# A two-layer fp32 trunk on one core: the first weights in six pieces on two DMA queues, and tiles that begin at multiples of 128 bytes

## The chip, the cores and the metric

One core of one Trainium2 chip runs the whole kernel. The metric is device microseconds of one execution, as the median of several runs. The core has a matmul engine (TensorE, "PE", with a weight loader "PEld"), VectorE ("DVE"), ScalarE ("ACT"), GpSimd ("POOL") and SyncE ("SP"), which here only issues DMAs. ACT and POOL issue some DMAs too; an engine works through its own instructions, DMA issues among them, in order.

## What is computed

The reference runs 512 tokens of width 1024 through two layers, in float32. Cut to what matters:

```python
def reference(x, ...):
    h = x
    for layer in range(2):
        mix = even_mixer(h, ...) if layer % 2 == 0 else odd_mixer(h, ...)
        h = layer_norm(ALPHA * h + mix, ...)
        h = layer_norm(ALPHA * h + conv_ffn(h, ...), ...)
    return h

def even_mixer(x, ...):
    q_a, k_a, v_a, z_a, b_a, a_a, q_b, k_b, v_b = split(x @ w_in)   # the gates b_a, a_a: 6 + 6 columns
    q_a, k_a, v_a = silu(causal_depthwise_conv(q_a, k_a, v_a))
    beta = sigmoid(b_a)
    g = -exp(a_log) * softplus(a_a + dt_bias)                       # then summed along each chunk
    o_a = rms_norm(gated_delta_rule(l2(q_a), l2(k_a), v_a, g, beta)) * silu(z_a)
    o_b = dilated_attention(q_b, k_b, v_b, rel_bias)
    return concat(o_a, o_b) @ w_out
```

The odd layer has differential attention and gated linear attention in place of these; each layer ends in a convolutional feed-forward (2816 wide).

## The kernel before, in words

Activations lie transposed in SBUF, 128 features by 512 tokens in each of eight blocks: `h` (float32) and its split into a high and a low half in a reduced format, `xh` and `xl` (their names in the trace too). Weights come as 216 units of 512 KB in HBM (`wts`), each 128 x 1024, that is eight blocks of 128 x 128. A unit is loaded into a raw buffer `wr` (three of them), cast on ACT into the high half `wh`, and DVE subtracts to get the low half `wl`. A product is then 8 x 3 matmuls into one PSUM bank `pd`: `xh*wh`, `xl*wh`, `xh*wl`.

Unit 0 holds the columns of the gates (64 of 128 wide, so it is loaded as 64 columns a block, 256 KB, and its low halves lie in the same tile `wh` beside the high ones). Units 1 to 3 are the key, query and value columns of the first head; unit 4 and up follow.

`setup` loads tokens and units 0 and 1 in pieces. `START` lists the pieces in order: `("x", a, e)` is token block a; `(u, a, e)` is blocks a to e of unit u. Before, all token pieces are issued by SP and all weight pieces by ACT. A second loop over the same list casts and subtracts piece by piece. Units 2 and 3 are asked for after that (`self.ask`, which issues on SP), then `par` (per-feature parameters) and `con` (constants, with the identity). Unit 3 goes into the raw buffer of unit 0, unit 4 into that of unit 1, unit 5 into that of unit 2, and so on: a load waits until DVE has made the low half of the unit that lay there.

`even` then interleaves the matmuls of units 0 and 1 block by block (`narrow` and `mm3`), so PE needs the token blocks one after another. After that come units 2, 3, ... (`tile_of`, 24 matmuls each). Beside them the gates' chain runs (`gates`): ACT copies the second gate rows out of PSUM, DVE adds the first; identity, Abs, Exp and Ln on ACT; a max-and-add on DVE; Exp on ACT; scaling and a scan on DVE; then four small transposes `pg` on PE. These lines record their instructions through one helper (L159 before), so they all carry its line. A framework's scheduler sets the order of each engine's instructions; DMAs of SP and ACT take eight completion semaphores in turn.

Scratch tiles of the two mixers (2 KB a partition, tags `x0`, `x1`, ...) come from a pool in which tiles lie one behind another in the order in which they are first asked for. In the kernel before, `idle` (4 bytes) and `par` (1984 bytes) shift what follows them by 32 and 96 bytes, and small tiles of the mixers shift the scratch behind them: in the even mixer scratch begins 32 or 96 bytes past a multiple of 128, in the odd one at a multiple or 64 past it. `h`, `xh`, `xl`, `wr`, `wh`, `wl` and the tiles of the feed-forward begin at multiples of 128 already.

Of the kernel before, what the change touches and what calls it, by code (L numbers as in the profile page):

```python
# [9 lines left out]
F32 = mybir.dt.float32  # L10
# [7 lines left out]
P = 128  # L18
S = 512
# [15 lines left out]
_NP = 0  # L35
# [23 lines left out]
for _n, _w in (("ident", 128), ("maskT", 128), ("nm1", 32), ("i32", 32), ("lm", 4 * 32), ("scan", 512),  # L59
# [30 lines left out]
EVEN_SEQ = "h0 h1 h2 h3 h4 h5 q00 v0 q01 v1 q02 v2 q10 q11 q12 z0 z1 z2 z3 z4 z5"  # L90
ODD_SEQ = "0D12G3abcd"

START = (("x", 0, 1), (0, 0, 4), ("x", 1, 2), (1, 0, 2), ("x", 2, 3), (1, 2, 5), ("x", 3, 4), (0, 4, 8), ("x", 4, 5),
         ("x", 5, 6), (1, 5, 8), ("x", 6, 7), ("x", 7, 8))
WARM = 8
LEAD = 3
AHEAD = 2
# [17 lines left out]
class Chain:  # L115
    def __init__(self, gen, ready, prio):
        self.gen, self.ready, self.prio, self.eng, self.end = gen, ready, prio, None, ready
# [48 lines left out]
class Scratch:  # L166


    def __init__(self, t, pool, n, more=None):
        self.t, self.pool, self.free, self.of = t, pool, list(range(n)), {}  # L170
        if more is not None:
            self.free += [(k, more) for k in range(more.shape[1])]

# [21 lines left out]
class Trunk:  # L195
# [14 lines left out]
    def setup(self):  # L210
        nc, tc, ctx = self.nc, self.tc, self.ctx
        self.keep = ctx.enter_context(tc.tile_pool(name="keep", bufs=1))
        self.wp = ctx.enter_context(tc.tile_pool(name="wp", bufs=1))
        self.psd = ctx.enter_context(tc.tile_pool(name="psd", bufs=4, space=PSUM))
        self.pss = ctx.enter_context(tc.tile_pool(name="pss", bufs=4, space=PSUM))
        keep = self.keep
        self.h = keep.tile([P, KD, S], F32, name="h")
        self.xh = keep.tile([P, KD, S], F32R, name="xh")
        self.xl = keep.tile([P, KD, S], F32R, name="xl")
        first = [(u, self.wtiles()) for u in (U_AB, U_AB + 1)]  # L220

        self.ones = keep.tile([P, P], F32, name="ones")
        nc.gpsimd.memset(self.ones, 1.0 / P)
        idle = keep.tile([P, 1], F32, name="idle")
        tc.keep_in_program_order(nc.scalar.copy(out=idle, in_=self.ones[:, 0:1]))
        for what, a, e in START:
            if what == "x":
                nc.sync.dma_start(self.h[:, a, :], self.xt[:, a, :])
            else:

                u, w = first[what]
                n = 64 if u in NARROW else P
                tc.keep_in_program_order(nc.scalar.dma_start(w[0][:, a * n : e * n], self.wts[u][:, a * n : e * n]))
        self.par = keep.tile([P, _NP], F32, name="par")
        self.con = keep.tile([P, _NCC], F32, name="con")

        warm = self.sps("warm")
        for _ in range(WARM):
            nc.tensor.matmul(warm[:, 0:P], lhsT=self.ones, rhs=self.ones, start=True, stop=True)
        self.onesL = keep.tile([P, P], F32, name="onesL")  # L240
        nc.gpsimd.memset(self.onesL, 1.0 / D)
        self.onesP, self.onesK = (keep.tile([P, P], F32R, name=f"ones{i}") for i in "PK")
        for x, n in ((self.onesP, P), (self.onesK, 512)):
            nc.vector.tensor_scalar(out=x, in0=self.ones, scalar1=P / n, scalar2=None, op0=ALU.mult)
        self.cst = keep.tile([P, 3], F32, name="cst")
        self.one, self.lneps, self.gdneps = (self.cst[:, i : i + 1] for i in range(3))
        nc.gpsimd.memset(self.one, 1.0)
        nc.gpsimd.memset(self.lneps, LN_EPS)
        self.rep = tc.dram_tile([4, P, L_TAB], F32, name="rep")
        self.chains, self.rec, self.asked = [], [], {}  # L250
        self.V, self.A = Eng(self, "DVE", nc.vector), Eng(self, "ACT", nc.scalar)
        self.G, self.T = Eng(self, "POOL", nc.gpsimd), Eng(self, "PE", nc.tensor)
        self.enter(EVEN)
        for what, a, e in START:
            if what == "x":
                hi, lo = self.xh[:, a, :], self.xl[:, a, :]
                nc.scalar.copy(out=hi, in_=self.h[:, a, :])
                nc.vector.tensor_tensor(out=lo, in0=self.h[:, a, :], in1=hi.bitcast(F32), op=ALU.subtract)
            else:
                u, w = first[what]  # L260
                self.split(u, *w, nc.scalar, nc.vector, slice(a * P, e * P))
        for u, w in first:
            self.pre[u] = w[1:]
        for u in (U_AB + 2, U_AB + 3):
            self.ask(u)
        nc.sync.dma_start(self.par, self.par_d)
        nc.sync.dma_start(self.con, self.con_d)
        self.ident = self.c("ident")
# [483 lines left out]
    def even(self):  # L752
        nc, tc = self.nc, self.tc
# [7 lines left out]
        def t1(n, w, bufs):  # L761
            return mp.tile([P, w], F32, name=self.nm(n), tag=n, bufs=bufs)

        self.enter(EVEN)
        g = {"zero": t1("zero", 1, 1)}
        seq = EVEN_SEQ.split()

        def of(x):
            a, i = x[0], int(x[1])
            if a == "h":  # L770
                return range(U_GDN + 3 * i, U_GDN + 3 * i + 3)
            if a == "q":
                u = U_SWA + 6 * i + 2 * int(x[2])
                return range(u, u + 2)
            if a == "v":
                return range(U_SWA + 12 + 2 * i, U_SWA + 14 + 2 * i)
            return range(U_Z + i, U_Z + i + 1)
# [101 lines left out]
        for x in seq:  # L879
            u, i = of(x)[0], int(x[1])  # L880
# [366 lines left out]
    def swa_pair(self, pair, taken, vts, bg, o, mp, t1):  # L1247
# [12 lines left out]
        for g in range(3):  # L1260
# [3 lines left out]
            for hh in range(2):  # L1264
# [3 lines left out]
                for n in range(NCH):  # L1268
                    w = 256 if g == 0 and n > 0 else P
                    if n == 0 or (g == 0 and n == 2):  # L1270
                        while X.room() < 1:
                            yield None
                        x = X.get("sc")
# [20 lines left out]
        def rows(cols, rw):  # L1294

            pr = self.sps("rows")
            T.transpose(out=pr[0:24, 0:P], in_=cols, identity=self.ident)
            tr = t1("tr", P, 2)
            V.tensor_copy(out=tr[0:24, :], in_=pr[0:24, 0:P])
            for hh in range(2):  # L1300
                G.dma_start(rw[hh : hh + 1, :], tr[12 * hh : 12 * hh + 12, :])
            yield 2500
# [5 lines left out]
        yield 0  # L1308
        rw = mp.tile([2, 3 * S], F32, name=self.nm("rw"), tag="rw", bufs=1)
        yield from rows(mx, rw)  # L1310
        while X.room() < 1:
            yield None
# [12 lines left out]
        for g in range(3):  # L1325
            for hh in range(2):
                for n in range(NCH):
                    ci = (g * NCH + n) * 2 + hh
                    li = hh * 12 + g * NCH + n
                    dst, k0, w = sc[g, hh][n]  # L1330
# [3 lines left out]
        for g in range(3):  # L1334
# [4 lines left out]
            for hh in range(2):  # L1339
                blocks = [(n, k0 // P + i, dst[:, i * P : (i + 1) * P]) for n in range(NCH)  # L1340
                          for dst, k0, w in (sc[g, hh][n],) for i in range(w // P)]
                for a in range(0, len(blocks), 4):
# [8 lines left out]
                    w = len(part) * P  # L1351
# [5 lines left out]
            for n in range(NCH):  # L1357
                for i in range(len(pts[0, n])):
                    for hh in range(2):
# [6 lines left out]
                        vt, f = (vts[g][pair], kb * P) if g else (vts[g][kb // 2], kb % 2 * HS + P * pair)  # L1366
# [5 lines left out]
        if pair:  # L1372
            X.put(*(x for v in vts for x in v))
        rw = mp.tile([2, 3 * S], F32, name=self.nm("rw"), tag="rw", bufs=1)
        yield from rows(ls, rw)
        while X.room() < 1:
            yield None
# [625 lines left out]
```

## Time and profile before

| | us |
|---|---|
| median of 3 runs (1410.32 to 1410.57) | 1410.34 |
| the profiled execution | 1412.89 |
| span in its trace, first to last instruction | 1411.1 |
| PE busy | 1385.7 |
| DVE busy | 839.3 |
| ACT busy | 673.5 |

The trace is of one execution, 2.55 us longer than the median of the runs. Busy times of PE count pipelined matmuls, each from its own start to its end, so a busy PE need not be at its peak; a step between starts is shorter than one matmul lasts.

### The profile page before, as it was taken

To read this page: it belongs to the slowest core of one execution; us is meant where nothing else is said; L and a number is where in the kernel's file an instruction comes from. 1 tells how busy PE (TensorE), PEld (TensorE's weight loads), DVE (VectorE), ACT (ScalarE), POOL (GpSimd) and SP (SyncE) were. 2 spreads that over 40 slices of the span, in tenths; PEclk is the share of its full clock that TensorE was granted. 3 is DMA by queue.
4 is the path that set the end of the run, shared out by engine and by line. 5 is a ranking of instruction groups with operands and counts; after the bars stand their busy time and mean duration, and the time that the engine had idled before them with its cause. 6 is when DMAs were issued, how large, how long until landed. Compare 5 with 4: busy or idle time off the path is not lost.

```text
span 1411.1 us, 22721 instructions
## 1 busy us (share of the span) xinstructions
PE 1385.7 (98%) x9050; PEld 1151.2 (82%) x9050; DVE 839.3 (59%) x1635; ACT 673.5 (48%) x1285; POOL 179.8 (13%) x237
## 2 busy tenths in 40 slices
PE   8999999999999999999999999999999999999997
PEld 6878787777798888888888977878898888888886
DVE  6876744544586555555243797777776555553354
ACT  6644433644857344434132755557565344432133
POOL 2103012011023111111010310000131111110010
PEclk9999999999999999999999999999999999999998
DMA  7434112121342322323233313211303322223221
GB/s 248 144 111 149 47 61 75 36 73 61 98 128 76 99 95 97 98 95 100 96 98 98 88 61 105 75 46 60 120 31 119 99 96 95 99 95 100 91 73 60
DMA packets 41457, 130.42 MB, mean 92 GB/s; under 512 B 4637, under 2 KB 9485, under 8 KB 41352
## 3 DMA queue, kind: packets, MB, share of 16 engines
q1 hardware_dynamic: 35584, 119.05, 26.1%
q10 hardware_dynamic: 4184, 4.92, 1.2%
q0 software_dynamic: 1584, 5.00, 1.1%
q8 instruction: 71, 1.16, 0.3%
q14 instruction: 34, 0.28, 0.1%
HBM read 126.76 MB, written 5.29 MB: 94 GB/s over the span
## 4 chain that ended last, share of the span: by engine, by line
PE 83%; DVE 6%; ACT 5%; DMA 3%; issue 2%; POOL 1%; ACTq 0%; DVEq 0%; POOLq 0%
PE pd L487 18%; PE pd L488 18%; PE pd L489 17%; PE pd L371 16%; PE pd L397 3%; DMA wr<-wts 2%; PE pc L159 1%; PE po L159 1%; PE sps L159 1%; PE pz L159 1%; PE py L159 1%; PE pa L159 1%; PE dsc L159 1%; DVE wl L159 1%; PE dpo L159 1%
## 5 line engine op out<-in xcount | busy, mean ns | idle before, releaser
L500 DVE TENSOR_TENSOR wl<-wr,wh 128x1024 fp32r<-128x1024 f32 (+1 forms) x153 | 187.9, 1229 | 301.8 <-ACT wh L499 298.7
L488 PE MATMUL pd<-xl,wh 128*128 128x512 f32 (+1 forms) x968 | 353.6, 366 | 0.2 <-DVE xl L684 0.2
L487 PE MATMUL pd<-xh,wh 128*128 128x512 f32 (+1 forms) x968 | 353.1, 366 | 0.4 <-ACT xh L683 0.4
L489 PE MATMUL pd<-xh,wl 128*128 128x512 f32 (+1 forms) x968 | 353.1, 365 | 0.0
L499 ACT CAST wh<-wr 128x1024 fp32r<-128x1024 f32 (+1 forms) x156 | 159.8, 1030 | 196.7 <-PE pd L488 171.4
L487 PEld LDWEIGHTS pd<-xh,wh 128*128 128x128 f32 x968 | 182.4, 189 | 30.4 <-ACT xh L683 0.9
L488 PEld LDWEIGHTS pd<-xl,wh 128*128 128x128 f32 x968 | 182.6, 189 | 30.1 <-DVE xl L684 1.1
L489 PEld LDWEIGHTS pd<-xh,wl 128*128 128x128 f32 x968 | 182.7, 189 | 29.5 <-issue 0.8
L371 PE MATMUL pd<-xh,wh 128*128 128x512 f32 x424 | 172.7, 407 | 0.0
L371 PE MATMUL pd<-xl,wh 128*128 128x512 f32 x424 | 170.9, 403 | 0.0
L487 PE MATMUL pd<-ah,wh 128*128 128x512 f32 (+1 forms) x396 | 145.1, 366 | 0.0
L489 PE MATMUL pd<-ah,wl 128*128 128x512 f32 (+1 forms) x396 | 144.7, 366 | 0.0
L488 PE MATMUL pd<-al,wh 128*128 128x512 f32 (+1 forms) x396 | 144.7, 365 | 0.0
L721 DVE SCALAR_TENSOR_TENSOR y<-pd,par,y 128x510 f32<-128x510 f32 (+1 forms) x176 | 130.4, 745 | 2.8
L371 PE MATMUL pd<-xh,wl 128*128 128x512 f32 x424 | 117.8, 402 | 0.0
L730 POOL TENSOR_TENSOR al<-y,ah 128x512 fp32r<-128x512 f32 x44 | 59.1, 1343 | 407.6 <-ACT ah L729 407.6
L159 DVE TENSOR_TENSOR wl<-wr,wh 128x1024 fp32r<-128x1024 f32 x63 | 77.1, 1224 | 42.6 <-PE pd L371 17.6
L159 ACT CAST wh<-wr 128x1024 fp32r<-128x1024 f32 x63 | 65.9, 1047 | 66.6 <-PE pd L371 48.2
L371 PEld LDWEIGHTS pd<-xl,wh 128*128 128x128 f32 x424 | 80.5, 190 | 16.2 <-issue 1.9
L371 PEld LDWEIGHTS pd<-xh,wh 128*128 128x128 f32 x424 | 80.4, 190 | 15.7 <-issue 0.3
L371 PEld LDWEIGHTS pd<-xh,wl 128*128 128x128 f32 x424 | 76.4, 188 | 14.6 <-issue 0.7
L487 PEld LDWEIGHTS pd<-ah,wh 128*128 128x128 f32 x396 | 74.7, 189 | 12.2
(387 smaller groups left out, 1868.6 us busy)
## 6 DMA issues: line engine op xcount, KB each, us to landing
wr<-wts SPq DMA_DIRECT2D x213, 512.0 KB, 3.4
h<-xt SPq DMA_DIRECT2D x16, 256.0 KB, 4.1
rep<-tab POOLq DMA_DIRECT2D x1, 3072.0 KB, 15.5
h<-gd POOLq DMA_DIRECT2D x6, 256.0 KB, 7.5
qe<-ge ACTq DMA_DIRECT2D x5, 256.0 KB, 4.4
bd<-rep ACTq DMA_DIRECT2D x1, 1024.0 KB
out<-h SPq DMA_DIRECT2D x2, 512.0 KB, 3.2
con<-con SPq DMA_DIRECT2D x1, 544.0 KB
```

The source lines that it names most:

```text
L159: r = fn(*a, **k)
L371: self.nc.tensor.matmul(ps, lhsT=w[part][:, k * P : (k + 1) * P], rhs=x[:, k, :], start=(i == 0), stop=(i == 23))
L397: self.nc.tensor.matmul(pss[b][:, a : a + n], lhsT=chunk(x[:, k, :], c), rhs=ws, start=(k == 0 and a == 0 and not part and x is self.xh), ...
L487: nc.tensor.matmul(ps, lhsT=wh, rhs=ah, start=first, stop=False)
L488: nc.tensor.matmul(ps, lhsT=wh, rhs=al, start=False, stop=False)
L489: nc.tensor.matmul(ps, lhsT=wl, rhs=ah, start=False, stop=last)
L499: A.copy(out=hi, in_=raw)
L500: V.tensor_tensor(out=lo, in0=raw, in1=hi.bitcast(F32), op=ALU.subtract)
L721: V.scalar_tensor_tensor(out=y[:, sft:], in0=ps[:, : S - sft], scalar=w(2 - sft), in1=y[:, sft:], op0=ALU.mult, op1=ALU.add)
L730: G.tensor_tensor(out=al[:, f, :], in0=y, in1=ah[:, f, :].bitcast(F32), op=ALU.subtract)
```

## The change

The list of pieces is cut anew: unit 0 comes in three pieces (blocks 0 to 2, 2 to 5, 5 to 8; before in two), unit 1 in three as before. The first three weight pieces (`FIRST`) stay on ACT's queue; the other three are issued by SP, between token pieces. `idle` goes; its one-element copy is written into a column of `cst`, which is made 32 wide and moved ahead; `par` is padded to 512 columns. The even and odd mixers' scratch tiles are all asked for once at the start of their pool, the `st` tiles of the even mixer too, so that small tiles lie behind them; `tr` has one buffer and not two.

```diff
-START = (("x", 0, 1), (0, 0, 4), ("x", 1, 2), (1, 0, 2), ("x", 2, 3), (1, 2, 5), ("x", 3, 4), (0, 4, 8), ("x", 4, 5),
-         ("x", 5, 6), (1, 5, 8), ("x", 6, 7), ("x", 7, 8))
+START = (("x", 0, 1), (0, 0, 2), ("x", 1, 2), (1, 0, 2), ("x", 2, 3), (0, 2, 5), ("x", 3, 4), (1, 2, 5), ("x", 4, 5),
+         (0, 5, 8), ("x", 5, 6), (1, 5, 8), ("x", 6, 7), ("x", 7, 8))
+FIRST = 3
...
+        for i in range(n):
+            pool.tile([P, S], F32, name=t.nm("x"), tag=f"x{i}", bufs=1)
...
-        idle = keep.tile([P, 1], F32, name="idle")
-        tc.keep_in_program_order(nc.scalar.copy(out=idle, in_=self.ones[:, 0:1]))
-        for what, a, e in START:
+
+        self.cst = keep.tile([P, 32], F32, name="cst")
+        tc.keep_in_program_order(nc.scalar.copy(out=self.cst[:, 8:9], in_=self.ones[:, 0:1]))
+        for i, (what, a, e) in enumerate(START):
...
-                tc.keep_in_program_order(nc.scalar.dma_start(w[0][:, a * n : e * n], self.wts[u][:, a * n : e * n]))
-        self.par = keep.tile([P, _NP], F32, name="par")
+                here = i < 2 * FIRST
+                d = (nc.scalar if here else nc.sync).dma_start(w[0][:, a * n : e * n], self.wts[u][:, a * n : e * n])
+                if here:
+                    tc.keep_in_program_order(d)
+        self.par = keep.tile([P, -(-_NP // 32) * 32], F32, name="par")[:, :_NP]
...
-        self.cst = keep.tile([P, 3], F32, name="cst")
...
+        for i in range(4):
+            t1(f"st{i}", P, 2)
...
-            tr = t1("tr", P, 2)
+            tr = t1("tr", P, 1)
```

SP's queue at the start of the program, before (tokens `xt`, then unit 2, the parameters, the constants, units 3 and 4):

```order
L228 DMA h<-xt 128x512 x8
L345 DMA wr_142<-wts 128x1024
L266 DMA par<-par 128x496
L267 DMA con<-con 128x1088
L345 DMA wr_146<-wts 128x1024
L345 DMA wr_221<-wts 128x1024
```

And SP's queue in the changed kernel, down to the same unit 4:

```order
L233 DMA h<-xt 128x512 x4
L239 DMA wr_73<-wts 128x384
L233 DMA h<-xt 128x512
L239 DMA wr_70<-wts 128x192
L233 DMA h<-xt 128x512
L239 DMA wr_73<-wts 128x384
L233 DMA h<-xt 128x512 x2
L352 DMA wr_144<-wts 128x1024
L352 DMA wr_148<-wts 128x1024
L273 DMA par<-par 128x496
L274 DMA con<-con 128x1088
L352 DMA wr_270<-wts 128x1024
```

Three weight pieces (`wr_70` is unit 0, `wr_73` unit 1) stand between the tokens, and unit 3 (`wr_148`) stands ahead of `par` and `con`. On ACT the second token cast now stands ahead of the first weight cast.

ACT during the gates' chain, before, from the casts of units 2 and 3 on (`pd_159` is the gates' product, `pd_160` unit 1's; `wh_222`, `wh_277` and `wh_312` are units 4 to 6):

```order
L159 CAST wh_143<-wr_142 128x1024
L159 CAST rp_660<-rb_659 33x4
L159 CAST wh_147<-wr_146 128x1024
L159 COPY h<-pd_159 38x512
L159 ACTIVATE h<-pd_160,par 128x512
L159 CAST wh_222<-wr_221 128x1024
L159 ACTIVATE h<-h,par 38x512
L159 CAST wh_277<-wr_276 128x1024
L159 ACTIVATE h<-h 38x512 x2
L159 CAST wh_312<-wr_311 128x1024
L159 ACTIVATE h<-h,cst 38x512
L159 ACTIVATE h<-h 38x512
```

The same stretch on ACT in the changed kernel (`wh_271`, `wh_326` and `wh_361` are units 4 to 6):

```order
L160 CAST wh_145<-wr_144 128x1024
L160 CAST wh_149<-wr_148 128x1024
L160 COPY h<-pd_208 38x512
L160 ACTIVATE al_259<-par 6x1
L160 ACTIVATE h<-pd_209,par 128x512
L160 ACTIVATE h<-h,par 38x512
L160 ACTIVATE h<-h 38x512
L160 CAST wh_271<-wr_270 128x1024
L160 ACTIVATE h<-h 38x512
L160 CAST wh_326<-wr_325 128x1024
L160 ACTIVATE h<-h,cst 38x512
L160 CAST wh_361<-wr_360 128x1024
```

The identity (`h<-h,par`) and the Abs behind it moved ahead of the cast of unit 4, Exp ahead of that of unit 5, Ln ahead of that of unit 6; the small `al` moved from ahead of unit 2's cast to behind the copy, and `rp` to among the tokens' casts.

DVE over the same stretch before, from the low half of unit 2 to the scaling that precedes the scan:

```order
L159 TENSOR_TENSOR wl_144<-wr_142,wh_143 128x1024
L159 TENSOR_TENSOR rp_660<-rb_659,rp_660 33x4
L159 TENSOR_TENSOR wl_148<-wr_146,wh_147 128x1024
L159 TENSOR_TENSOR h<-pd_159,h 38x512
L159 SCALAR_TENSOR_TENSOR h<-pd_160,par,h 128x511
L159 TENSOR_TENSOR wl_223<-wr_221,wh_222 128x1024
L159 SCALAR_TENSOR_TENSOR h<-pd_160,par,h 128x510
L159 TENSOR_TENSOR wl_278<-wr_276,wh_277 128x1024
L159 SCALAR_TENSOR_TENSOR h<-pd_160,par,h 128x509
L159 TENSOR_TENSOR wl_313<-wr_311,wh_312 128x1024
L159 SCALAR_TENSOR_TENSOR h<-h 38x512
L159 TENSOR_SCALAR h<-h,al_210 6x512
```

And DVE in the changed kernel:

```order
L160 TENSOR_TENSOR wl_146<-wr_144,wh_145 128x1024
L160 TENSOR_TENSOR wl_150<-wr_148,wh_149 128x1024
L160 TENSOR_TENSOR h<-pd_208,h 38x512
L160 SCALAR_TENSOR_TENSOR h<-pd_209,par,h 128x511
L160 SCALAR_TENSOR_TENSOR h<-pd_209,par,h 128x510
L160 SCALAR_TENSOR_TENSOR h<-pd_209,par,h 128x509
L160 TENSOR_TENSOR wl_272<-wr_270,wh_271 128x1024
L160 TENSOR_TENSOR wl_327<-wr_325,wh_326 128x1024
L160 SCALAR_TENSOR_TENSOR h<-h 38x512
L160 TENSOR_TENSOR wl_362<-wr_360,wh_361 128x1024
L160 TENSOR_SCALAR h<-h,al_259 6x512
```

The three convolution steps stand together ahead of the low halves of units 4 and 5, and the max-and-add (`h<-h`) ahead of that of unit 6. On PE one more matmul of unit 3 stands behind `pg`, six and not five. Behind this stretch the order on every engine is as before.

## Rows read from the trace of the kernel before

**Rows 1.** The page's busy times: us, share of the span, instructions.

```profile
PE 1385.7 (98%) x9050; PEld 1151.2 (82%) x9050; DVE 839.3 (59%) x1635; ACT 673.5 (48%) x1285; POOL 179.8 (13%) x237
```

**Rows 2.** Chain of waits, 0 to 40 us: start us, us, what.

```profile
0.75 3.24 DMA h<-xt
...
11.15 6.13 DMA wr<-wts
...
19.63 4.19 DMA wr<-wts
...
29.34 0.41 PE pg L159 x4
```

**Rows 3.** Timeline, 4 to 8 us: start us, us, engine, line, operation; idle before.

```profile
4.01 1.36 ACTq L233 DMA_DIRECT2D wr<-wts  x2
5.42 0.62 ACT L257 CAST xh<-h 128x512 fp32r<-128x512 f32 x1 [3.19 <-DMA h<-xt]
...
7.16 0.79 PE L507 MATMUL pd<-xh,wh 128*128 128x512 f32 x1 [2.37 <-DVE wh L500]
```

**Rows 4.** Windows: busy us of PE, PEld, DVE, ACT, POOL; granted clock; DMA; GB/s.

```profile
27.80:29.30 1.50, 0.02 (x1) 0.00 (x0) 1.40 (x2) 0.61 (x1) 0.00 (x0) 1.00 0.70 270
...
30.90:34.30 3.40, 3.40 (x9) 2.65 (x9) 2.98 (x5) 1.59 (x3) 2.96 (x6) 0.50 0.39 105
...
222.70:224.40 1.70, 0.00 (x0) 0.00 (x0) 0.00 (x0) 1.01 (x4) 1.29 (x3) 1.00 0.68 229
```

**Rows 5.** Timeline of PE, 21 to 35 us.

```profile
21.54 1.98 PE L371 MATMUL pd<-xh,wl 128*128 128x512 f32 x8
...
30.98 0.63 PE L371 MATMUL pd<-xh,wh 128*128 128x512 f32 x1
...
34.35 0.40 PE L371 MATMUL pd<-xh,wh 128*128 128x512 f32 x1
```

**Rows 6.** Issues at 1.19, 6.78, 7.63, 8.10 us: KB, us to landing.

```profile
h<-xt SPq DMA_DIRECT2D x1, 256.0 KB, 3.8
...
h<-xt SPq DMA_DIRECT2D x1, 256.0 KB, 4.6
...
h<-xt SPq DMA_DIRECT2D x1, 256.0 KB, 5.1
...
wr<-wts SPq DMA_DIRECT2D x1, 512.0 KB, 5.9
```

**Rows 7.** Timeline of ACT and DVE during the gates' chain, 13 to 30 us.

```profile
13.50 1.28 ACT L413 ACT_TABLE_LOAD   x1
...
18.38 1.23 DVE L159 TENSOR_TENSOR wl<-wr,wh 128x1024 fp32r<-128x1024 f32 x1 [0.99 <-ACT wh L159]
...
19.52 0.68 DVE L159 TENSOR_TENSOR h<-pd,h 38x512 f32<-38x512 f32 x1
19.57 1.04 ACT L159 CAST wh<-wr 128x1024 fp32r<-128x1024 f32 x1
...
20.51 0.82 ACT L159 ACTIVATE h<-h,par 38x512 f32<-38x512 f32 x1
...
22.16 1.30 ACT L159 ACTIVATE h<-h 38x512 f32<-38x512 f32 x2
...
27.51 0.48 DVE L159 TENSOR_SCALAR h<-h,al 6x512 f32<-6x512 f32 x1 [0.70 <-ACT h L159]
```

**Rows 8.** Groups by form, DVE and PE: busy us, mean ns; idle before.

```profile
L721 DVE SCALAR_TENSOR_TENSOR y<-pd,par,y 128x511 f32<-128x511 f32 x88 | 65.2, 743 | 0.0
...
L159 DVE SCALAR_TENSOR_TENSOR qkv<-pd,par,qkv 128x511 f32<-128x511 f32 x10 | 7.4, 741 | 0.0
...
L159 PE MATMUL pk<-con,qkv 128*128 128x128 f32 x12 | 1.8, 272 | 0.0
L159 PE MATMUL pk<-con,h 128*128 128x128 f32 x12 | 1.8, 272 | 0.0
```

**Rows 9.** Waits of SP's queue, 0 to 60 us: us, times, longest.

```profile
SPq L228 <- DMA h<-xt: 3.7, 1, 3.7
```

## What I expect, and why

> **What bounds the kernel now.** I read the page first: TensorE (PE) is busy for 1385.7 of 1411.1 us [rows 1]. So the kernel is bound by PE's work, and a change that leaves PE's matmuls as they are can only win where PE waits or runs at the lower clock. The change rewrites the first loads, so I read the timeline of the first 8 us next. The first token piece lands at 3.99 us (issued at 0.75, 3.24 long) [rows 2], yet its cast starts on ScalarE (ACT) at 5.42 [rows 3]: the two DMA issues of 4.01 to 5.37 stand ahead of it in ACT's queue, and they had to wait for a landing themselves. PE's first matmul starts at 7.16, behind the low half of the first weights on VectorE (DVE) [rows 3].
>
> Then the chain of waits up to 40 us. The reader should see that it doesn't run through PE after 7.16: it runs through a load issued at 11.15 (unit 3, which needs the raw buffer of unit 0) that takes 6.13 us, a second one from 19.63, and ends at the four small transposes `pg` at 29.34, the gates of the delta rule [rows 2]. PE has its work ready long before: between 27.80 and 29.30 it is busy for 0.02 us. And behind that wait the granted clock is 0.50 (1.2 GHz instead of 2.4) from 30.90 to 34.30 [rows 4]. There eight matmuls start over 3.37 us (30.98 to 34.35), against steps of (1.98-0.39)/7 = 0.227 us at the full clock [rows 5]: 8 x 0.227 = 1.81, so the lower clock costs 1.56 us. Start, wait and lower clock are what this change can reach.
>
> **The change, part by part.**
>
> *First pieces.* ACT now issues three DMAs, none of which waits, and is free for the cast when the token piece lands, at 4.0 instead of 5.42. Not all of these 1.4 us arrive: ACT now casts two token pieces before the first weights, and the second one lands about 0.9 us after the first (1.19 + 3.8 = 5.0) [rows 6]. Cast of piece 1 from 5.0 to 5.6, a weight cast and its low half on DVE, both for half the columns of before, some 0.3 each and a little queueing: first matmul at about 6.55, 0.6 earlier. PE is then at its lower clock, as in the start before, and I don't know that the clock rises earlier; if it rises when it did, the 0.6 us buy about 1.4 matmuls at 0.42, worth 1.4 x 0.227 = 0.3. I take 0.5 us for PE's place at the end of units 0 and 1, between 0.3 and 0.6.
>
> *The rest between the tokens.* Three weight pieces move to SP's queue, each between token pieces, so the sum of bytes up to the last token piece is the same, and I let that piece land where it did, at 7.63 + 5.1 = 12.7, and unit 2 at 8.10 + 5.9 = 14.0 [rows 6]. PE needs the last token piece, whose low half is then ready at 14.0, for the last 8 of the 40 matmuls of units 0 and 1; the 32 ahead of them take 32 x 0.227 and 0.2 more for each of some nine at the lower clock, 9.1 us, so to 15.6. That is 1.6 us of cover. One more DMA is issued than before; its fixed part is covered by the transfers ahead of it.
>
> *Units 2 and 3 ahead of the parameters.* In SP's new order unit 3 comes before `par` and `con` (792 KB together); before, it came behind them. Token pieces of 256 KB land 0.65 us apart (6.78 + 4.6 = 11.4 and 7.63 + 5.1 = 12.7, two steps) [rows 6], so 512 KB are 1.3 us: unit 3 lands at about 15.3 (its buffer is free at about 10.9, much as before) instead of 11.15 + 6.13 = 17.28. `par` and `con` come at about 16.0 and 17.4; the first to read `par` now stands behind the gates' copy on ACT, at 17, so they delay nobody.
>
> *The gates' chain.* Now the new order on ACT and DVE, walked with steps of before [rows 7]: a full cast holds ACT for 0.94 (19.57 to 20.51), a low half holds DVE for 1.14 (18.38 to 19.52) and starts as its cast ends, 1.04 plus a little behind its start. Last token cast done at 13.3; table load 1.28, to 14.6; casts of units 2 and 3 from 14.6 and 15.5; the gates' copy at 16.5. DVE: low halves from 15.7 and 16.8, the gates' sum at 17.95 (19.52 before), ready at 18.6. ACT: identity 0.82, to 19.4; Abs 0.65, to 20.1; cast of unit 4; Exp from 21.0; cast of unit 5 from 21.7; Ln from 22.6; cast of unit 6 from 23.3, done at 24.35. DVE: low half of unit 5 from 22.8, the max-and-add at 23.9, low half of unit 6 from 24.5, the scaling from 25.65. From there the scan and the transposes followed 1.83 us later (27.51 to 29.34): `pg` at 27.5, 1.84 earlier. The loads that this needs: unit 6 takes unit 3's buffer at 17.95 and lands 4.19 later [rows 2], at 22.1, before 23.3; so it is no longer what ACT waits for.
>
> *What PE gets of it.* One matmul of unit 3 moves from before `pg` to behind it. PE's last matmul before `pg` ended at 27.8; now 0.5 (start) + 0.23 (that matmul) earlier, 27.1. So a wait of 0.4 us is left of 1.5. What counts: `pg` 1.84 earlier, less 0.23 for the matmul now behind it, 1.61 us. And with the wait gone from 1.5 to 0.4 us I expect that the clock stays up: 1.56 us more. Sum 3.17 us.
>
> *Later.* The order on every engine is the same after the gates' chain, so PE's lead of 1.6 to 3.2 us is kept unless a wait of PE begins at something that did not move. Nothing after the first loads starts from the clock: casts, low halves and later loads all follow a buffer or a result that PE gives, and move with it. So I let the lead last to the end.
>
> *128-byte starts.* `par`, `con`, the small ones and the 2 KB scratch tiles began 32, 64 or 96 bytes past such a multiple; tokens, weights and the FFN's tiles, which PE streams most, began at one already. The trace has both kinds side by side: the convolution step on DVE into scratch `qkv` (off) takes 741 ns, the same step into the FFN's `y` (on) 743; PE's transposes `pk` take 272 ns from `qkv` and 272 from pieces of `h` (on) [rows 8]. So I cost this part at nothing; 2 ns on each of a hundred such instructions would be 0.2 us either way, my bound.
>
> **The sum.** The profiled execution took 1412.89 us with a span of 1411.1; the runs have a median of 1410.34, 2.55 less. 1412.89 - 3.17 = 1409.72 for a profiled one, 1410.34 - 3.17 = **1407.2 us** for the median. 0.2% is 2.8 us, about what a measurement of this kernel can tell from no change.
>
> **The rivals.**
>
> *A, forecast: chain and clock.* 1407.2, from 1406.7 (PE does not wait at all: 0.5 + 1.51 + 1.56 = 3.6) to 1407.6.
>
> *B: the chain moves, the clock doesn't help.* At 222.70 PE idled for the whole of 1.70 us and the clock stayed at 1.00 behind it [rows 4], so an idle stretch of this length doesn't always lower it. Either the fall at 30.90 has another cause and comes again, or it is not in the unprofiled runs, which are 2.55 us shorter than the profiled one. Then only 1.61 is left: 1408.7, within 0.2%.
>
> *C: the wait takes it all.* If unit 3 lands no earlier than 17.3 (the DMAs share one set of engines, and what is first in SP's queue need not land first), its cast starts at 17.3 and the chain follows as before, with `pg` at about 28.9 to 29.3. PE's earlier start then only lengthens the wait: 1410.1.
>
> *D, slower: SP's queue runs dry.* A DMA on SP waits for the landing of one issued eight earlier; before, SP's sixth token piece stood 3.7 us in that wait [rows 9]. Now seven more issues stand in such waits, and smaller pieces keep fewer bytes in flight. A load into an empty queue takes 3.24 us from issue to landing [rows 2], in a filled one it adds 0.65: each time the queue empties costs 2.6. The Trainium skill, page "SBUF — State Buffer", section "The DMA setup-cost knee", says of this that every DMA pays about 2 us that don't grow with its bytes, and advises one large transfer rather than several; by that figure, an estimate, one exposed piece would cost 2 us. The landings 0.65 us apart show that here these parts overlap while the queue is filled. The tokens have some 1.6 us of cover, the chain 1.6; emptied once the time is about as before or 1 us above, emptied twice 2 x 2.6 - 1.6 = 3.6 above: 1413.9. It decides from about 4.4 us of lost transfer on. Against it: when SP can issue the sixth token piece, about 6.6 us, a token piece, 192 KB of unit 1, another token piece and 96 KB of unit 0 are still on the way, 800 KB, or 2.0 us at the measured spacing.
>
> **How the numbers follow.** A 0.42, B 0.29, C 0.20, D 0.09. A lies around the bound: 0.36 of it beyond 2.8 us, the rest within; of B some 0.04 (a chain better than walked) goes to faster. D is split between slower (0.07) and same. So faster 0.40, same 0.53, slower 0.07. The range leaves out D and the best end of A: 1405.9 to 1410.5; A's own is 1406.7 to 1407.6.
>
> **What would show it.** First cast at 4.0 and first matmul at 6.4 to 6.7; the cast of unit 3 before 16; the gates' copy at 16.5 and their sum on DVE at 18.0 and not 19.5; `pg` between 27 and 28 with under 0.8 us of idle PE before it; a clock of 1.00 from 30 to 34 us; from 40 us on the same groups with the same means, `qkv` and `pk` among them. The prediction is wrong where a token cast waits for its DMA beyond 13.5, where PE waits between 7 and 18 us, where the clock falls again, or where PE's lead at 40 us is not there any more at 400.

## The result, and the profile after

The change made the kernel slower: a median of 1423.97 us (1422.82 to 1424.99, 4 runs) against 1410.45 us of the kernel before (1410.32 to 1410.70, 4 runs), a ratio of 1.0095 with a 95% interval of 1.0078 to 1.0113. I had said 1407.2 us, with 1405.9 to 1410.5 as the range. The profiled execution took 1424.99 us. One run of experiment 11 took 3514.26 us, where the other eleven took 1409.63 to 1412.26; it is in no time or ratio given here.

The page of the changed kernel, busy us of the engines: beside [rows 1] only PE has changed, from 1385.7 to 1399.7, with as many matmuls. PE does not wait longer; its work has become longer.

```profile
span 1423.2 us, 22725 instructions
...
PE 1399.7 (98%) x9050; PEld 1150.8 (81%) x9050; DVE 840.0 (59%) x1636; ACT 673.5 (47%) x1286; POOL 180.2 (13%) x237
```

The start first, since the prediction was about it. Timeline of the changed kernel, 3.5 to 8 us (start us, us, engine, line, operation; idle before):

```profile
3.86 0.62 ACT L264 CAST xh<-h 128x512 fp32r<-128x512 f32 x1 [1.63 <-DMA h<-xt]
...
5.93 0.62 ACT L264 CAST xh<-h 128x512 fp32r<-128x512 f32 x1 [1.45 <-DMA h<-xt]
6.45 0.60 ACT L506 CAST wh<-wr 128x128 fp32r<-128x128 f32 x2
...
7.53 0.80 PE L514 MATMUL pd<-xh,wh 128*128 128x512 f32 x1 [3.11 <-DVE wh L507]
```

The first cast starts at 3.86 and not at 5.42 [rows 3], as foreseen. But the second token cast stands ahead of the first weight cast and waits for a piece that lands at 5.91, and the first matmul comes at 7.53, later than before (7.16). Then the windows that answer to [rows 4], and PE's timeline at the gates' transposes:

```profile
7.29:10.71 3.42, 3.18 (x8) 2.30 (x9) 2.66 (x7) 2.33 (x7) 0.00 (x0) 0.50 1.06 334
...
27.80:29.30 1.50, 1.50 (x10) 1.00 (x9) 0.03 (x1) 1.37 (x2) 0.00 (x0) 1.00 0.96 367
30.90:34.30 3.40, 3.40 (x16) 2.75 (x15) 2.86 (x5) 1.06 (x3) 2.81 (x6) 1.00 0.41 118
...
221.80:223.40 1.60, 0.00 (x0) 0.00 (x0) 0.00 (x0) 0.96 (x4) 1.19 (x3) 1.00 0.73 236
```

```profile
28.27 0.43 PE L160 MATMUL pg<-con,h 38*128 38x38 f32 x4
```

`pg` starts at 28.27 (29.34 before, [rows 2]), without a wait; the clock from 30.9 to 34.3 us is 1.00 where it was 0.50, with 16 matmuls instead of 9. In this execution PE had the lower clock earlier instead, at 0.50 from 7.29 to 10.71 us, over its first matmuls; ahead of them it had stood idle for 3.11 us. So far the changed kernel is ahead, and the long wait of 222.70 before [rows 4] ends some 0.9 us earlier.

But the lead melts. A row of eight matmuls like the one in [rows 5], which took 1.98 us before, takes 2.02 in the changed kernel's timeline of PE:

```profile
45.00 2.02 PE L378 MATMUL pd<-xh,wl 128*128 128x512 f32 x8
```

(2.02 - 0.39)/7 = 0.233 us from start to start, instead of 0.227. The groups by form show for the whole program which matmuls these are. The kernel before (mean ns of one; PE's matmuls overlap, so one lasts longer than a step):

```profile
L488 PE MATMUL pd<-xl,wh 128*128 128x512 f32 x744 | 289.9, 390 | 0.2 <-DVE xl L684 0.2
L489 PE MATMUL pd<-xh,wl 128*128 128x512 f32 x744 | 289.8, 390 | 0.0
L487 PE MATMUL pd<-xh,wh 128*128 128x512 f32 x744 | 289.2, 390 | 0.4 <-ACT xh L683 0.4
...
L488 PE MATMUL pd<-al,wh 128*128 128x512 f32 x308 | 119.8, 389 | 0.0
```

And the changed kernel:

```profile
L495 PE MATMUL pd<-xl,wh 128*128 128x512 f32 x744 | 293.9, 396 | 0.2 <-DVE xl L691 0.2
L496 PE MATMUL pd<-xh,wl 128*128 128x512 f32 x744 | 293.9, 395 | 0.0
L494 PE MATMUL pd<-xh,wh 128*128 128x512 f32 x744 | 293.2, 396 | 0.4 <-ACT xh L690 0.4
...
L495 PE MATMUL pd<-al,wh 128*128 128x512 f32 x308 | 119.8, 389 | 0.0
```

Every matmul that streams the tokens (`xh`, `xl`) over a weight tile takes 5 to 6 ns more, at the full clock and without a wait; those that stream `ah` and `al` over the same weight tiles (the second half of the feed-forward) take 389 as before. The three groups alone hold 12.1 us more than before (881.0 against 868.9).

What differs between these two kinds is where their tiles begin, counted from the sizes of the tiles ahead of them. The small tiles lie behind the tokens and ahead of the weights. Before, `idle`, `par` and `cst` took 32 + 1984 + 32 = 2048 bytes; now `cst` and `par` take 128 + 2048 = 2176. So all that lies behind, the weights, `ah`, `al` and the other FFN tiles, begins 128 bytes higher, and `h`, `xh` and `xl`, which lie ahead, stay. In 256 bytes, tokens and weights both began at 128 before; now tokens begin at 128 and weights at 0. `ah` and `al` moved together with the weights. The theory to test: PE's step depends on the distance between the tile that it streams and the tile from which its weights are loaded, and the diff changed that distance for the tokens. The rivals: START, that the new order of first loads sets a rhythm on PE that never settles; SCRATCH, that the tiles which now begin at multiples of 128 cost; ABSOLUTE, that weights at a multiple of 256 are slow wherever the tokens lie.

### The profile page after: what moved, and what is told of

Same layout as the page of the kernel before. It is cut to its first block, busy times and chain, and to the rows that moved or that the text cites. A ratio compares the mean times of both kernels' runs of the same rounds, so it can differ in the third digit from the quotient of the medians.

```text
span 1423.2 us, 22725 instructions
## 1 busy us (share of the span) xinstructions
PE 1399.7 (98%) x9050; PEld 1150.8 (81%) x9050; DVE 840.0 (59%) x1636; ACT 673.5 (47%) x1286; POOL 180.2 (13%) x237
## 4 chain that ended last, share of the span: by engine, by line
PE 86%; DVE 6%; ACT 3%; DMA 2%; issue 2%; POOL 1%; ACTq 0%; SPq 0%; POOLq 0%; DVEq 0%
PE pd L495 19%; PE pd L494 19%; PE pd L496 19%; PE pd L378 15%; PE pd L404 3%; PE pc L160 1%; PE po L160 1%; PE sps L160 1%; PE pz L160 1%; PE py L160 1%; PE dsc L160 1%; PE pa L160 1%; DVE wl L160 1%; DVE h L160 1%; PE dpo L160 1%
## 5 line engine op out<-in xcount | busy, mean ns | idle before, releaser
L495 PE MATMUL pd<-xl,wh 128*128 128x512 f32 (+1 forms) x968 | 357.6, 370 | 0.2 <-DVE xl L691 0.2
L494 PE MATMUL pd<-xh,wh 128*128 128x512 f32 (+1 forms) x968 | 356.8, 370 | 0.4 <-ACT xh L690 0.4
L496 PE MATMUL pd<-xh,wl 128*128 128x512 f32 (+1 forms) x968 | 357.1, 369 | 0.0
L506 ACT CAST wh<-wr 128x1024 fp32r<-128x1024 f32 (+2 forms) x157 | 159.6, 1023 | 207.9 <-PE pd L495 183.7
L495 PEld LDWEIGHTS pd<-al,wh 128*128 128x128 f32 x396 | 74.7, 189 | 12.1
```

Source lines behind the costliest of these rows:

```text
L494: nc.tensor.matmul(ps, lhsT=wh, rhs=ah, start=first, stop=False)
L495: nc.tensor.matmul(ps, lhsT=wh, rhs=al, start=False, stop=False)
L496: nc.tensor.matmul(ps, lhsT=wl, rhs=ah, start=False, stop=last)
L506: A.copy(out=hi, in_=raw)
```

## The experiments

The kernel before was timed again on the same chip in each set of runs; its medians were 1410.76, 1411.57, 1410.65 and 1410.35 us. In the diffs, `keep` is the pool that holds tokens and small tiles.

**1. Only the distance, in the kernel before.**

```diff
+        keep.tile([P, 32], F32, name="gap")
...
-            tr = t1("tr", P, 2)
+            tr = t1("tr", P, 1)
```

> The kernel before with an unused 128-byte tile behind the last small tile (room made by one buffer for the scratch `tr`, instead of two): every weight tile, FFN tile and scratch tile begins 128 bytes higher, the tokens h, xh and xl stay; the order of the work is that of before. Theory (the distance between the token tile that is streamed and the weight tile decides PE's step, and it is now off by 128 in 256): step of the matmuls on xh and xl 230 to 235 ns instead of 227, those on ah and al stay at 227, time 1421 to 1426 us. Rival START (the new order of first loads sets a phase that never settles): steps 227, 1410.4. Rival SCRATCH (the tiles moved to multiples of 128 cost): they are off again here, so 1410.4.

Measured: 1423.70 us (1423.25 to 1424.29, 4 runs), ratio 1.0088, 1.0074 to 1.0102. An empty tile of 128 bytes costs all that the change cost. The groups by form of this kernel:

```profile
L489 PE MATMUL pd<-xl,wh 128*128 128x512 f32 x744 | 293.7, 395 | 0.2 <-DVE xl L685 0.2
...
L489 PE MATMUL pd<-al,wh 128*128 128x512 f32 x308 | 119.9, 389 | 0.0
```

START and SCRATCH fall: neither is in this kernel. (The one buffer for `tr` is in experiment 2 as well, which is fast.)

**2. The changed kernel, distance as before.** The `gap` line of experiment 1 added to it.

> The changed kernel with an unused 128-byte tile behind the last small tile: weights, FFN tiles and scratch begin 128 bytes higher than in the changed kernel, all still at multiples of 128, so that the weights stand at the same place in 256 bytes as before the change. Theory (distance tokens to weights): steps back at 227 ns, the 13 us are gone and the gain at the start is left, 1407.5 to 1409.5 us. Rival START: steps stay at 232, 1423 to 1425. Rival SCRATCH: 1423 to 1425.

Measured: 1410.51 us (11 runs), ratio 0.9997, 0.9988 to 1.0006. The loss is gone, and with it the gain that I expected at the start: it is not there. The group by form, and the row of eight:

```profile
L496 PE MATMUL pd<-xl,wh 128*128 128x512 f32 x744 | 289.6, 390 | 0.2 <-DVE xl L692 0.2
```

```profile
43.96 1.98 PE L379 MATMUL pd<-xh,wl 128*128 128x512 f32 x8
```

**3. Only the new first loads, in the kernel before** (`START`, `FIRST` and the choice of the queue from the diff; no tile moves).

> The kernel before with the new order of first loads alone; every tile stays where it was. Theory: steps 227 ns; what the start gives alone, 1407.5 to 1409.5 us, the wait ahead of the gates' transposes gone. Rival START: steps 232 ns, 1421 to 1425. Rival SCRATCH: as the theory here.

Measured: 1411.00 us (11 runs), ratio 1.0000, 0.9992 to 1.0009, and groups of 390 to 391 ns. The steps are those of the theory, and again there is no gain.

**4. Tokens and weights both moved.**

```diff
+        keep.tile([P, 32], F32, name="gap0")
         self.h = ...
...
+        keep.tile([P, 32], F32, name="gap")
```

> The changed kernel with 128 unused bytes ahead of the tokens and 128 behind the last small tile: tokens 128 and weights 256 bytes higher than in the changed kernel. The weights keep their place in 256 bytes (that of the slow kernel), the tokens now share it. Theory (distance): steps 227 ns, 1407.5 to 1409.5 us. Rival ABSOLUTE (weights that begin at a multiple of 256 are slow wherever the tokens are): steps 232, 1422 to 1426. Rival START: 1422 to 1426.

Measured: 1410.51 us (11 runs), ratio 0.9992, 0.9983 to 1.0001, and groups of 390:

```profile
L497 PE MATMUL pd<-xl,wh 128*128 128x512 f32 x744 | 289.8, 390 | 0.2 <-DVE xl L693 0.2
```

The weights begin at the same place in 256 bytes as in the slow kernel and are fast, since the tokens do too. ABSOLUTE falls.

**5. The kernel before once more,** for its start.

> The kernel before, unchanged, profiled a second time, to see what of its start belongs to every execution. If the wait of 1.51 us ahead of the gates' transposes and the lower clock from 30.9 to 34.3 us belong to the kernel, both are there again. Rival: they belong to one execution (the place of the first landings and of the clock's steps differs from run to run): no fall of the clock at 31 us, a wait under 1 us, and a time near 1410.5 instead of 1412.9.

Measured: 1411.01 us (1 run). The windows and the chain of waits of this execution of the same kernel:

```profile
27.80:29.30 1.50, 1.37 (x9) 0.86 (x7) 1.23 (x2) 0.91 (x1) 0.00 (x0) 1.00 0.91 306
30.90:34.30 3.40, 3.40 (x17) 2.79 (x16) 3.22 (x5) 1.42 (x3) 3.13 (x6) 1.00 0.45 111
```

```profile
29.03 0.13 issue
29.16 0.41 PE pg L159 x4
```

`pg` comes at 29.16, much as in [rows 2], but PE waits 0.13 us for it and not 1.5, and the clock stays at 1.00. So the wait and the fall of the clock, on which my sum rested, are not in every execution of this kernel. Nor are they confined to the one that I had read: in experiments 7 and 8 PE waits 1.67 and 1.61 us ahead of `pg`, and the granted clock is 0.50 from 28.87 to 32.28 and from 29.22 to 32.63, while in experiment 2 a wait of 1.51 us is followed by no fall. Of the 61 runs of the kernel before that were timed beside the experiments, 5 took over 1412.5 us.

**6, 7, 9, 10. Other distances.** The `gap` of experiment 2, with `[P, 16]` (64 bytes), `[P, 48]` (192), `[P, 24]` (96) and `[P, 40]` (160).

> The changed kernel with 64 unused bytes behind the last small tile: weights at 64 in 256, tokens at 128. Theory HALVES (what counts is whether both begin in the same 128-byte half of 256): steps 232 ns, 1422 to 1425 us. Theory GRADED (the step grows with the distance): steps 228 to 230 ns, 1414 to 1419. Theory EXACT (any distance that isn't a multiple of 256 is slow): 1422 to 1425.

> The same with 192 unused bytes: weights at 192 in 256, tokens at 128, the distance is 64 to the other side. HALVES: 227 ns, 1409.5 to 1411.5 us. GRADED: 228 to 230 ns, 1414 to 1419. EXACT: 1422 to 1425.

> The changed kernel with 96 unused bytes behind the last small tile: weights at 96 in 256, tokens at 128, weights 32 bytes below. So far, weights less tokens in 256: 0 gave 1410.5 us, +64 gave 1426.1, 128 gave 1423.9, -64 gave 1416.1. If the step is a smooth function of the distance with its least value at 0: 1411 to 1414 us. If its least value lies a little below 0: under 1410, and this version beats both kernels. If what counts is only that both share a 64-byte piece: as -64, 1416.

> The same with 160 unused bytes: weights 32 bytes above the tokens' place in 256. Smooth with the least value at 0: between 0 and +64, 1413 to 1422 us. If both only have to share a 64-byte piece (128 to 191): 1410.5.

Measured, with those above, by where the weights begin less where the tokens begin, in 256 bytes; the means are those of the `xl` and `al` rows of the groups by form. The sets were timed on different chips, so compare the ratios, each to the kernel before on the same chip:

| weights less tokens | kernel | median us | ratio (95%) | xl ns | al ns |
|---|---|---|---|---|---|
| 0 | before; 2; 4 | 1410.5 to 1410.8 | 0.9997; 0.9992 | 390 | 389 |
| +32 | 10 | 1426.96 | 1.0115 (1.0102 to 1.0128) | 397 | 389 |
| +64 | 7 | 1426.06 | 1.0101 (1.0086 to 1.0116) | 396 | 389 |
| 128 | changed; 1 | 1423.97; 1423.70 | 1.0095; 1.0088 | 396; 395 | 389 |
| -64 | 6 | 1416.05 | 1.0027 (1.0015 to 1.0039) | 394 | 389 |
| -32 | 9 | 1425.58 | 1.0105 (1.0092 to 1.0118) | 396 | 389 |

None of my three rules held: not halves (+64 shares one and is slow), not a smooth growth (32 bytes off is as bad as 128 on either side), and for "exact" -64 is too fast. The later guesses fell too: a least value a little below 0 (-32 is slow), and one shared 64-byte piece (+32 shares it and is slow). What holds is that 0 is the one good distance of the six, and that a sign matters at 64. In the kernels of this table `ah` and `al` began at 0, 64, 96, 128, 160 or 192 in 256, always with their weights, and never left 389.

**8. The same on other tiles.** Experiment 2, and in each feed-forward:

```diff
+            fp.tile([P, 32], F32, name=f"gapa{layer}")
             ah = fp.tile([P, NF, S], F32R, name=f"ah{layer}")
             al = fp.tile([P, NF, S], F32R, name=f"al{layer}")
+            fp.tile([P, 32], F32, name=f"gapb{layer}")
```

> The changed kernel with the 128 bytes behind the small tiles (fast in the second experiment), and in each FFN 128 unused bytes ahead of ah and 128 behind al, so that ah and al now begin 128 bytes off their weights, and nothing else changes its distance. Theory (distance of any streamed tile to its weights): the matmuls on ah and al now take steps of 231 to 233 ns instead of 227, those on xh and xl stay at 227; 1056 matmuls of 512 columns at 5.5 more are 5.8 us: 1415 to 1417.5 us. Rival (something peculiar to the token tiles, their place or their writers): all steps 227, 1410.5.

Measured: 1417.82 us (5 runs), ratio 1.0041, 1.0027 to 1.0055. Now `al` is slow and `xl` is not, in the groups by form:

```profile
L496 PE MATMUL pd<-xl,wh 128*128 128x512 f32 x744 | 289.7, 390 | 0.2 <-DVE xl L692 0.2
...
L496 PE MATMUL pd<-al,wh 128*128 128x512 f32 x308 | 121.7, 395 | 0.0
```

The theory named the matmuls. Against the kernel before on the same chip (1411.57 us) the price is 6.2 us by the medians and 5.8 by the ratio, with 3.8 to 7.8 as its interval; I had 5.8. The 7.3 us that the expectation of experiment 12 uses is the distance to experiment 2, which ran on another chip.

**12. Only the low halves of the weights.** Experiment 2, with 128 unused bytes between the `wh` and the `wl` tiles and 128 behind.

> The changed kernel with the 128 bytes behind the small tiles (fast), and 128 unused bytes ahead of the four wl tiles and 128 behind them: only the low halves of the weights now begin 128 off the tiles that are streamed over them, for xh and ah alike; wh, the tokens, ah, al and the weights of out_proj keep their distance. Theory OWN PAIR (a matmul is slow where its own weights are off): the steps of the matmuls with wl, one in three, become 231 to 234 ns or take most of the loss. Theory NEXT WEIGHTS (the load of the next matmul's weights beside the running stream): the steps of the matmuls on xl and al, which run while wl is loaded, take the loss. Either way about a third of what shifting all costs: (13.4 + 7.3) / 3 = 6.9 us, 1417 us. Rival (only a shift of all weights disturbs the rhythm): 1410.5.

Measured: 1424.53 us (4 runs), ratio 1.0101, 1.0084 to 1.0118: 14.2 us over the kernel before on this chip, twice what I had said. The groups by form:

```profile
L503 PE MATMUL pd<-xh,wl 128*128 128x512 f32 x744 | 295.6, 398 | 0.0
L502 PE MATMUL pd<-xl,wh 128*128 128x512 f32 x744 | 294.9, 397 | 0.2 <-DVE xl L698 0.2
L501 PE MATMUL pd<-xh,wh 128*128 128x512 f32 x744 | 289.5, 391 | 0.4 <-ACT xh L697 0.4
```

Of the three matmuls of a block two are slow: the one whose own weights `wl` are off, and the one ahead of it, whose own pair (`xl` over `wh`) is in place but which runs while `wl` is loaded. The mixers check the second half. There 16 matmuls of `xh` and `xl` over `wh` alternate and the eight over `wl` come at the end, so that only the last `xl` of a unit runs while `wl` is loaded. Their groups in experiment 2 and here:

```profile
L379 PE MATMUL pd<-xl,wh 128*128 128x512 f32 x424 | 169.9, 401 | 0.0
...
L379 PE MATMUL pd<-xh,wl 128*128 128x512 f32 x424 | 117.5, 401 | 0.0
```

```profile
L379 PE MATMUL pd<-xl,wh 128*128 128x512 f32 x424 | 170.1, 401 | 0.0
...
L379 PE MATMUL pd<-xh,wl 128*128 128x512 f32 x424 | 118.7, 404 | 0.0
```

`xl` over `wh` stays at 401 where no `wl` is loaded beside it. OWN PAIR and NEXT WEIGHTS each name one of the two slow kinds and miss the other. Two kinds of three instead of one explain most of the doubled price, not all of it: two thirds of what both shifts together cost would be (13.5 + 6.2) x 2/3 = 13.1 us, and the two kinds are 7 to 8 ns slower here, against 5 to 6 in the changed kernel.

**11. PE's first matmul as early as can be.** Experiment 2, with ACT's first five casts held in the order of `START` (`A` casts through `tc.keep_in_program_order` for the first five pieces).

> The changed kernel with the 128 bytes behind the small tiles, and ScalarE's first five casts held in the order of the first loads, so that the first weights are cast ahead of the second token piece (in the changed kernel they stand behind it and wait for its landing); with it the gates' copy moves ahead of unit 3's cast. First matmul at 5.2 to 5.6 us in every execution, and not at 6.1 to 7.8. If the start is bound by PE's first matmuls: 1.0 to 1.5 us less than the second experiment, 1409.0 to 1409.5. If it is bound by the gates' chain and PE only waits longer ahead of the gates' transposes: 1410 to 1410.8.

Measured: 1411.42 us (11 runs), ratio 1.0004, 0.9995 to 1.0012: no gain. PE's timeline:

```profile
5.52 0.50 PE L517 MATMUL pd<-xh,wh 128*128 128x512 f32 x1 [0.73 <-DVE wh L510]
...
27.84 0.41 PE L160 MATMUL pg<-con,h 38*128 38x38 f32 x4 [1.07 <-issue]
```

The first matmul is at 5.52, 1.6 us earlier than before, and PE stands 1.07 us ahead of `pg`. With experiment 2, where PE began at 6.13 and waited 1.51 for a `pg` at 27.15, this shows in two executions that the gates' chain bounds the start when PE begins early. In the profiled executions:

| kernel | token piece 1 lands | first matmul | `pg` | idle ahead of it | time of this execution |
|---|---|---|---|---|---|
| before [rows 2 to 4] | 5.02 | 7.16 | 29.34 | 1.5 | 1412.89 |
| before, again | 5.05 | 7.18 | 29.16 | 0.1 | 1411.01 |
| changed | 5.91 | 7.53 | 28.27 | 0 | 1424.99 |
| experiment 2 | 4.51 | 6.13 | 27.15 | 1.5 | 1410.68 |
| experiment 3 | 6.15 | 7.77 | 28.94 | 0 | 1411.00 |
| experiment 4 | 5.50 | 7.13 | 27.71 | 0.2 | 1408.81 |
| experiment 11 | 6.11 | 5.52 | 27.84 | 1.1 | 1409.63 |

## Why the prediction was wrong

**The step that failed: "128-byte starts", costed at nothing with 2 ns on a hundred instructions as its bound.** I asked what the change does to the tiles that it puts at multiples of 128, and there the answer held: the convolution step into `qkv` takes 743 ns in the changed kernel (741 in [rows 8]). I wrote that tokens, weights and the FFN's tiles "began at one already", and took that for a reason to leave them out. But padding small tiles moves everything that lies behind them, and the places of tokens and weights to each other changed under the matmuls that bound the kernel. The loss is 5 to 6 ns on the 2232 matmuls of the three groups shown, 12.1 us, and some 3 ns on the 1272 of the mixers (the group with `xl` has 401 ns in experiment 2 and 404 in the changed kernel), 3.8 us: 15.9 at most, where 13.5 were measured. That the rest falls where PE waits for other engines in the mixers anyway is likely, not shown. My bound was made from the wrong instructions: a term that touches PE's 9050 matmuls needs a bound from them. With 1 ns on each it would have been 9 us, and the range would have had to reach past 1410.5 on that side.

**First pieces: place right, size wrong.** The cast started at 3.9 (4.0 predicted). The first matmul was to come at 6.55; it came at 6.13 in experiment 2 and at 7.13 to 7.77 in the changed kernel and in experiments 3 and 4, since the second token piece, which I let land at 5.0, landed at 4.5 or at 5.5 to 6.2. The casts' order was in my sum; that its landing can be so late was not.

**The rest between the tokens: right.** SP's queue did not run dry; in the changed kernel's chain and its issues the last token piece, issued at 7.95, landed at 12.5 (12.7 predicted), and nowhere between 7.5 and 18 us does PE wait over 0.15 us. Rival D fell. The estimate from the Trainium skill, page "SBUF — State Buffer", section "The DMA setup-cost knee", that each exposed piece would cost 2 us was not put to the test: no piece was exposed.

**Unit 3 and the gates' chain: right, and a little late.** Unit 3, issued at 11.50, landed 4.7 us later, at 16.2 (15.3 predicted, 17.28 before); the gates' sum on DVE stood at 18.49 (17.95 predicted). `pg` came at 27.2 to 28.4 in the six executions with the new order in which PE waited for it (experiments 2, 4, 7, 8, 9 and 11; 27.5 predicted), 0.8 to 2.2 us earlier than in the two executions of the kernel before.

**The clock and the wait: taken from one execution.** Of my 3.17 us, 1.56 were a lower clock, 1.1 a shorter wait ahead of `pg` (0.4 instead of 1.51), and 0.5 PE's own earlier place. The second execution of the same kernel has no lower clock there and a wait of 0.13 us, so that little of the first two terms was there to be gained. Rival B named this for the clock ("or it is not in the unprofiled runs, which are 2.55 us shorter than the profiled one"), and I subtracted the terms from the median of those runs all the same. Experiments 2 and 3 give 1410.51 and 1411.00 against 1410.76, which is nothing within intervals of some 1.3 us either way. Experiment 4, the best version here, is at 0.9992 with an interval that still takes in 1; so no run shows a version that surely beats the kernel before.

**Later: wrong at its root.** The order of the work was the same, as I had said. But "from 40 us on the same groups with the same means" is the sentence by which the prediction asked to be judged, and 390 became 396. The other half of this step, "So I let the lead last to the end", failed as well where the steps were those of before. PE's last matmul ahead of `py`, a group of small products of the delta rule, and `py` itself, in experiment 2 and then in experiment 5:

```profile
71.82 0.39 PE L379 MATMUL pd<-xl,wh 128*128 128x512 f32 x1
73.93 0.74 PE L160 MATMUL py<-xx,lt 32*32 32x32 f32 x64 [1.72 <-DVE uu L160]
```

```profile
73.19 0.39 PE L371 MATMUL pd<-xl,wh 128*128 128x512 f32 x1
74.13 0.74 PE L159 MATMUL py<-xx,lt 32*32 32x32 f32 x64 [0.55 <-DVE uu L159]
```

Experiment 2 is 1.37 us ahead of experiment 5 before this wait, and 0.20 us ahead after it. Its chain of waits comes there from the gates, over DMAs that carry them out and back (`gd<-h` from 27.14, `h<-gd` from 30.28 to 36.43 us), and then mostly over DVE. So in this execution the gates' chain does not end at `pg`, where my sum ended it. In experiment 4 this wait is 0.55 us, as in experiment 5, and `py` comes at 72.86; that execution took 1408.81 us. How often an execution keeps such a lead, two traces can't tell; the medians show no gain.

Left open: why only equal places in 256 bytes are fast (the fast distances that were run are two, 256 bytes apart), why -64 costs less than +64, why in experiment 12 the matmul behind the load of a shifted `wl` is slow too, and by which part of PE the loads of weights and the stream meet. The traces show their starts and ends alone.

## What to carry to other kernels

Before a change to the sizes or the order of small tiles is called free, list where the tiles begin that PE streams and those that hold its weights, before and after; here equal places in 256 bytes kept the step at 227 ns, and 128 unused bytes at the right place undid a loss of 13.5 us. Bound a term by the instructions that the edit can reach, also through addresses, and not by those that it names. And a wait or a fall of the clock that is to be subtracted from a median should stand in a second execution as well, above all where the profiled one is longer than the median by nearly as much as the two together.

## What the runs showed of the hardware

In this kernel's fp32r matmuls of 128 x 512 outside the mixers, a group's mean is 389 to 391 ns, and a step 227, where streamed tile and weight tile begin at the same place in 256 bytes, and 392 to 397 where they don't. What matters is the distance: moving both left the mean alone, for tokens and weights in experiment 4 and for `ah` and `al` at the six places of the table. The Trainium skill, page "SBUF — State Buffer", section "A bandwidth-pool intuition that's wrong (but worth ruling out)", gives PE a second, independent read port for the loads of its weights. The runs differ from what that suggests: in experiment 12 a matmul whose own tiles were in place took 397 ns instead of 390 while weights from a shifted tile were loaded beside it. The measurement decides here: in this kernel the two reads are not independent in time.
